# Mixer LayerNorm: fifth up chunk split ahead of the first normalization, the third tile's steps put between the h2 rests, rotary key of all tiles at once

## The chip, the cores and the metric

The kernel runs on one core of one Trainium2 chip. Its time is the device time of one execution in microseconds (us), the median of several runs. Before the change it is 981.97 us (3 runs, 981.78 to 982.18). The core has a matrix engine (PE, with its weight loads shown apart as PEld), a vector engine (DVE), a scalar engine (ACT), GpSimd (POOL), and SyncE (SP), which issues most of the loads. Each engine runs its own instructions strictly in order and waits on semaphores for the others.

## The reference, cut to what matters

One layer of a streaming encoder on a sequence of 512 positions and 1024 channels, all in float32:

```
h = layer_norm(x) * (1 + sc_t) + sh_t
y = token_mixer(h)              # pooling, latent attention and spatial gating, gated, merged, @ w_o
x = layer_norm(ALPHA * x + gt_t * y) * ln_t_g + ln_t_b      # "mixer's LayerNorm"
h = layer_norm(x) * (1 + sc_f) + sh_f                       # called h2 in the kernel
z = h @ w_up                    # 1024 -> 2 * 2816, then a convolution over 3 positions
y = (silu(gate) * val) @ w_down
x = layer_norm(ALPHA * x + gt_f * y) * ln_f_g + ln_f_b
```

sh, sc and gt come from a product of silu(c) with a weight w_ada. In the attention, a key of 64 channels per position (kr) is turned by rotary angles: the first half times cos minus the second times sin, and so on.

## The kernel before, in words

**Numbers.** A float32 product is made of three passes of a faster format: every operand a is split into a "high" part (ah, a cast on ACT) and a "rest" (al = a - ah, on DVE or POOL), and PE adds al*bh, ah*bl and ah*bh. Names end in h and l for the two. `wsplit` (L92, L93) does it for a weight chunk of 128x1024, `mm3` (L106 to L108) does the three products of one tile, `mm_chunk` (L113, L114, L116) those of a chunk of eight tiles. The 512 positions are four tiles t of 128 rows; the 1024 channels of h and h2 are eight column tiles j.

**Order.** A scheduler orders each engine's instructions from the program's order and estimated times. Where the order matters the code pins it: `tc.issue_after(ins)` keeps what follows behind an instruction, and `in_turn` chains steps on DVE one after another around the mixer's LayerNorm.

**Three places matter here.**

*Rotary key* (L549 to L603). After the first projection, for each tile t: ACT squares the latent columns (L553, L554), POOL takes the power -1/2 of the sums (`power`, L130 and L133, twice per tile), ACT scales by it (cn, L558, L559), DVE multiplies the key by cos and sin (tA, tB, L565, L568), and POOL makes the rotated key ro (L571, L572), its high part twice (L574, L575) and its rest (L576) in a tile kr of its own. Then PE transposes cn (ptc, L585) and kr (ptk, L597, L601) and begins the rotary queries (pq, L106 to L108).

*Row gate gt_t* (`ada_rows`, L815 to L829, called at L895). The modulation row gt_t is summed on DVE by `ada_piece` during the eight merges of the first branch. `ada_rows` splits the two sums (ACT L821, POOL L822) and lets PE spread each over all rows with two products (pgt, L827); DVE adds a bias row (L828), which SP loads. It is called right before the pooling products (pmx). The spatial gating's products follow, `uv_half(2)` and `uv_half(3)` (tiles pu, L929 to L932).

*Mixer's LayerNorm* (L1114 to L1345). `project_out` makes y for tile after tile (accumulators pyo) and calls `after_mixer(t)` behind each. For a tile: `residual` (DVE, adds ALPHA*x, takes statistics, L1196 to L1201), `centre` (L1208), `scale` (L1216), `second_stats` (the statistics for h2, DVE L153 and L142, then three small POOL steps, L130, L133, L145, that give rs), `second_norm` (ACT, xr, L1229). PE turns xr (`turn`, tiles pth, L1241), two tiles t at a time: the first pair's turns stand among the products of the fourth tile. `second_modulation(tp, jp)` makes two column tiles of h2 for a pair tp: ACT the high parts (h2T0h to h2T7h, L1260) and a full copy (h2f, L1263), DVE the rests (h2T0l to h2T7l, L1269).

Meanwhile the first six chunks of w_up are split early: `early_split(m)` casts (ACT, L1174; names uph, wuph), `early_low(m)` makes the rest (DVE, L1180; upl, wupl). `up_early` then multiplies these six chunks by the first pair of tiles (256 positions) as soon as h2 is there (tiles pzu, 128x256), and later by the second pair; the other 38 chunks follow in whole (128x512).

In `after_mixer` before, the fifth chunk (m = 4) is cast on ACT behind the second tile's xr, and its rest on DVE stands behind the second tile's statistics; the third tile's three steps come before the first rest h2T0l.

Of the kernel before, what the change touches and what calls it, by code (L numbers as in the profile page):

```python
# [8 lines left out]
F32 = mybir.dt.float32  # L9
F32R = mybir.dt.float32r  # L10
# [9 lines left out]
TT = 4  # L20
# [30 lines left out]
def trunk(ctx: ExitStack, tc: tile.TileContext, A, out):  # L51
# [498 lines left out]
    krs = []  # L550
    for t in range(TT):
        sq = pad_t("sq")
        nc.scalar.activation(sq[:, 0:256], lat[t][:, 0:256], AF.Square, accum_out=ss[:, t, 0:1])  # L553
        nc.scalar.activation(sq[:, 256:384], lat[t][:, 256:384], AF.Square, accum_out=ss[:, t, 1:2])  # L554
        power(rr[:, t, 0:1], ss[:, t, 0:1], 1.0 / 256.0, RMS_EPS, 1)
        power(rr[:, t, 1:2], ss[:, t, 1:2], 1.0 / 128.0, RMS_EPS, 1)
        cn = pt_t(f"cn{t}")
        nc.scalar.activation(cn[:, 0:256], lat[t][:, 0:256], AF.Copy, scale=rr[:, t, 0:1])  # L558
        nc.scalar.activation(cn[:, 256:384], lat[t][:, 256:384], AF.Copy, scale=rr[:, t, 1:2])  # L559
        cqn.append(cn)  # L560
        ro = sm.tile([P, 64], F32, name="ro", tag="ro", bufs=2)
        tA = sm.tile([P, 2, 32], F32, name="tA", tag="tA", bufs=2)
        tB = sm.tile([P, 2, 32], F32, name="tB", tag="tB", bufs=2)
        src = lat[t][:, 384:448].rearrange("p (a b) -> p a b", a=2)
        nc.vector.tensor_tensor(  # L565
            out=tA, in0=src, in1=cosT[:, t : t + 1, :].broadcast_to([P, 2, 32]), op=ALU.mult
        )
        nc.vector.tensor_tensor(  # L568
            out=tB, in0=src, in1=sinT[:, t : t + 1, :].broadcast_to([P, 2, 32]), op=ALU.mult
        )  # L570
        nc.gpsimd.tensor_tensor(out=ro[:, 0:32], in0=tA[:, 0, :], in1=tB[:, 1, :], op=ALU.subtract)  # L571
        nc.gpsimd.tensor_tensor(out=ro[:, 32:64], in0=tA[:, 1, :], in1=tB[:, 0, :], op=ALU.add)  # L572
        kr = act_t(f"kr{t}", F32)
        nc.gpsimd.tensor_copy(out=kr[:, 0:64].bitcast(F32R), in_=ro)  # L574
        nc.gpsimd.tensor_copy(out=kr[:, 64:128], in_=kr[:, 0:64])  # L575
        nc.gpsimd.tensor_tensor(out=kr[:, 128:192], in0=ro, in1=kr[:, 0:64], op=ALU.subtract)  # L576
        krs.append(kr)
    for m in range(2, 4):
        th0.append(gate(0, m))
    cT_hi = []  # L580
# [13 lines left out]
    krL = m_t("krL", F32R)  # L594
    pt = ps("ptk")
    for t in range(TT):
        nc.tensor.transpose(pt[:, t * P : (t + 1) * P], krs[t][:, 0:128], ident)  # L597
    nc.scalar.copy(out=krT, in_=pt)
    pt = ps("ptk")
    for t in range(TT):  # L600
        nc.tensor.transpose(pt[0:64, t * P : (t + 1) * P], krs[t][:, 128:192], ident)  # L601
    nc.vector.tensor_copy(out=krL[0:64, :], in_=pt[0:64, :])
    nc.gpsimd.memset(f(krL[64:128, :]), 0.0)  # L603

# [285 lines left out]
    for m in range(KT):  # L890
# [1 line left out]
            pool(m + 1)  # L892
        merge(0, m, oT_hi, oT_lo, th0[m])
        behind_split(ada_piece, 0, m)
    gt_t = ada_rows(0, 0, "gtt")  # L895

    mx_hi = []
    mx_lo = []
    for g in range(4):
# [43 lines left out]
        nc.vector.bn_stats(out=stv[:, q, 0, :], in_=v0[q])  # L943

    v0 = uv_half(2, "v", lambda q: behind_split(ada_piece, 1, q))
    v1 = uv_half(3, "v", lambda q: behind_split(v_second, q))
    shf = ada_cols(1, C_SHF, False, "shf")
    gsg = row_tiles(6, pt_t, "gsg")
# [282 lines left out]
            )  # L1231

    turned = {}

    def turn(tp, jp):
        pt = ps("pth")
# [10 lines left out]
    def second_modulation(tp, jp):  # L1247
        tt_ = slice(2 * tp * P, (2 * tp + 2) * P)
        pt = turned.pop((tp, jp))
        full = pad_t("h2f")  # L1250
        for jj in range(2):
            j = 2 * jp + jj
            c = slice(jj * 256, (jj + 1) * 256)
            if tp and jj:
                nc.vector.tensor_scalar(
                    out=h2_hi[j][:, tt_], in0=pt[:, c], scalar1=scf[:, j : j + 1],
                    scalar2=shf[:, j : j + 1], op0=ALU.mult, op1=ALU.add,
                )
            else:
                nc.scalar.activation(  # L1260
                    h2_hi[j][:, tt_], pt[:, c], AF.Identity, bias=shf[:, j : j + 1], scale=scf[:, j : j + 1]
                )
            nc.scalar.activation(  # L1263
                full[:, c], pt[:, c], AF.Identity, bias=shf[:, j : j + 1], scale=scf[:, j : j + 1]
            )
        for jj in range(2):
            j = 2 * jp + jj
            c = slice(jj * 256, (jj + 1) * 256)
            ins = nc.vector.tensor_tensor(  # L1269
                out=h2_lo[j][:, tt_], in0=full[:, c], in1=f(h2_hi[j][:, tt_]), op=ALU.subtract  # L1270
            )
        return ins
# [259 lines left out]
```

## Time and profile before

| what | value |
|---|---|
| median of 3 runs | 981.97 us |
| the profiled execution | 979.05 us |
| its span (first to last instruction) | 977.2 us |
| granted TensorE clock, mean over the span | 0.992 |
| PE busy | 957.4 us, 98% |
| DVE, ACT, POOL busy | 588.8, 388.8, 291.1 us |
| HBM read | 116.30 MB |

The profile is one execution. In a timeline a row gives start, duration, engine, line, operation, output and inputs, shape, and in brackets how long the engine sat idle before it and what ended that idle time. Matmul durations are modelled ends of pipelined work and overlap; the distance between two starts is what a matmul costs. The chain of work that ended last lies 85% on PE, 5% on DVE, 4% on POOL and 2% on ACT.

### The profile page before, as it was taken

How to read it: one execution, taken by the hardware profiler on the slowest of the kernel's cores; microseconds unless marked ns; L12 is line 12 of the kernel's file. 1: busy time of each engine (PE TensorE's matmuls, PEld its weight loads, DVE VectorE, ACT ScalarE, POOL GpSimd, SP SyncE). 2: the span in 40 equal slices, each digit the busy share in tenths (PEclk: the TensorE clock that was granted, in tenths of full speed). 3: DMA queues.
4: the chain of work that ended last, by engine and by line, in shares of the span. 5: the costliest groups of instructions: out<-in, count | busy, mean ns of one | idle time of the engine just before them, and what ended most of it. 6: DMA issues, size and time to landing. Idle time of an engine off the chain costs nothing.

```text
span 977.2 us, 12237 instructions
## 1 busy us (share of the span) xinstructions
PE 957.4 (98%) x4566; PEld 805.0 (82%) x4566; DVE 588.8 (60%) x899; ACT 388.8 (40%) x654; POOL 291.1 (30%) x295
## 2 busy tenths in 40 slices
PE   8999999999999999999999998999999999999996
PEld 7888888888878888888888887988888888888885
DVE  6958657546785665656533486595555565632367
ACT  4575656533233322422323235364444444422121
POOL 3773122122440031302012721121111121755654
PEclk9999999999999999999999999999999999999998
DMA  9712112134445533364243450034343433333222
GB/s 334 287 62 85 51 40 81 52 130 151 134 135 183 178 123 101 120 235 171 66 118 120 132 192 22 23 129 129 108 130 108 134 125 94 119 112 107 86 87 87
DMA packets 45708, 119.20 MB, mean 122 GB/s; under 512 B 5329, under 2 KB 8785, under 8 KB 45649
## 3 DMA queue, kind: packets, MB, share of 16 engines
q1 hardware_dynamic: 45216, 118.25, 37.2%
q8 instruction: 36, 0.59, 0.2%
q10 hardware_dynamic: 432, 0.17, 0.1%
q14 instruction: 24, 0.19, 0.1%
HBM read 116.30 MB, written 2.10 MB: 121 GB/s over the span
## 4 chain that ended last, share of the span: by engine, by line
PE 85%; DVE 5%; POOL 4%; ACT 2%; issue 2%; DMA 2%; DVEq 0%; POOLq 0%; SPq 0%
PE pzu L113 7%; PE pzu L114 7%; PE pzu L116 7%; PE pg L113 4%; PE py L113 4%; PE pg L114 4%; PE pg L116 4%; PE py L114 4%; PE py L116 4%; PE pyd L1138 3%; PE pyd L1135 3%; PE pyd L1137 3%; PE pu L932 3%; PE pu L931 3%; PE pu L929 3%; PE lat L508 2%
## 5 line engine op out<-in xcount | busy, mean ns | idle before, releaser
L93 DVE TENSOR_TENSOR wupl<-wup,wuph 128x1024 fp32r<-128x1024 f32 x38 | 48.2, 1269 | 71.0 <-PE pzu L116 44.7
L1104 POOL TENSOR_TENSOR d<-d,gtfb 128x512 f32<-128x512 f32 x44 | 73.9, 1700 | 37.6 <-DMA d<-in_wdn 35.8
L1386 POOL TENSOR_TENSOR zc<-zc 128x512 f32<-128x512 f32 x22 | 29.8, 1356 | 172.2 <-ACT zc L1385 152.6
L1109 DVE TENSOR_TENSOR dl<-d,dh 128x1024 fp32r<-128x1024 f32 x18 | 28.7, 1594 | 56.2 <-PE pyd L1135 50.9
L410 POOL TENSOR_TENSOR mg<-mg,th 128x512 f32<-128x512 f32 x16 | 31.3, 1958 | 92.5 <-DVE th L407 92.4
L92 ACT CAST wuph<-wup 128x1024 fp32r<-128x1024 f32 x38 | 39.9, 1050 | 46.5 <-PE pzu L114 46.5
L93 DVE TENSOR_TENSOR wgl<-wg,wgh 128x1024 fp32r<-128x1024 f32 x22 | 27.9, 1268 | 42.2 <-ACT wgh L92 29.5
L92 ACT CAST wbh<-wb 128x1024 fp32r<-128x1024 f32 x24 | 25.3, 1054 | 69.3 <-PE py L114 50.2
L809 DVE SCALAR_TENSOR_TENSOR ada<-adar,cact,ada 128x512 f32<-128x512 f32 x56 | 49.6, 917 | 0.8 <-DMA adar<-in_ada 0.8
L1108 ACT CAST dh<-d 128x1024 fp32r<-128x1024 f32 x18 | 19.0, 1053 | 62.5 <-PE pyd L1138 37.6
L1368 ACT ACTIVATE zc<-pzu,cols 128x512 f32<-128x512 f32 x44 | 34.2, 779 | 21.2 <-PE pzu L116 17.0
L92 ACT CAST wgh<-wg 128x1024 fp32r<-128x1024 f32 x22 | 23.3, 1057 | 40.3 <-PE pg L114 27.1
L93 DVE TENSOR_TENSOR wsgl<-wsg,wsgh 128x1024 fp32r<-128x1024 f32 x16 | 19.6, 1225 | 31.7 <-ACT wsgh L92 28.2
L93 DVE TENSOR_TENSOR wbl<-wb,wbh 128x1024 fp32r<-128x1024 f32 x24 | 30.5, 1271 | 9.7 <-ACT wbh L92 5.5
L92 ACT CAST wsgh<-wsg 128x1024 fp32r<-128x1024 f32 x16 | 16.9, 1053 | 48.6 <-PE pu L932 44.1
L1371 DVE SCALAR_TENSOR_TENSOR zc<-pzu,cols,zc 128x511 f32<-128x511 f32 x44 | 32.6, 743 | 4.1 <-ACT zc L1368 4.1
L730 POOL TENSOR_SCALAR pe<-pe,mx 128x128 f32<-128x128 f32 (+3 forms) x32 | 17.1, 537 | 54.9 <-DVE mx L729 54.5
L1375 DVE SCALAR_TENSOR_TENSOR zc<-pzu,cols,zc 128x510 f32<-128x510 f32 x44 | 32.6, 744 | 0.8
L1385 ACT ACTIVATE zc<-zc 128x512 f32<-128x512 f32 x22 | 13.9, 631 | 40.5 <-DVE zc L1375 40.4
L407 DVE SCALAR_TENSOR_TENSOR th<-th,py 128x512 f32<-128x512 f32 x16 | 11.0, 686 | 30.9 <-PE py L116 30.9
L862 POOL TENSOR_TENSOR asum<-apad 128x527 f32<-128x527 f32 x8 | 12.2, 1520 | 55.4 <-ACT apad L857 29.3
L294 DVE SCALAR_TENSOR_TENSOR acc<-ada,cact,acc 128x512 f32<-128x512 f32 (+1 forms) x27 | 26.9, 1011 | 0.7
(1431 smaller groups left out, 3138.3 us busy)
## 6 DMA issues: line engine op xcount, KB each, us to landing
wup<-in_wup SPq DMA_DIRECT2D x44, 512.0 KB, 3.6
adar<-in_ada SPq DMA_DIRECT2D x64, 256.0 KB, 3.9
wb<-in_wb SPq DMA_DIRECT2D x24, 512.0 KB, 3.6
wg<-in_wg SPq DMA_DIRECT2D x22, 512.0 KB, 3.6
d<-in_wdn SPq DMA_DIRECT2D x22, 512.0 KB, 3.6
wsg<-in_wsg SPq DMA_DIRECT2D x16, 512.0 KB, 3.7
ada<-in_ada1p SPq DMA_DIRECT2D x24, 256.0 KB, 5.0
x<-in_x SPq DMA_DIRECT2D x16, 256.0 KB, 3.4
```

Of the source, the lines that this page charges most:

```text
L92: nc.scalar.copy(out=hi[:, :n], in_=raw[:, :n])
L93: ins = nc.vector.tensor_tensor(out=lo[:, :n], in0=raw[:, :n], in1=f(hi[:, :n]), op=ALU.subtract)
L113: nc.tensor.matmul(o, wh[:, c], xl[k], start=k == 0, stop=False)
L114: nc.tensor.matmul(o, wh[:, c], xh[k], start=False, stop=False)
L116: nc.tensor.matmul(o, wl[:, c], xh[k], start=False, stop=k == KT - 1)
L410: nc.gpsimd.tensor_tensor(out=merged[m], in0=merged[m], in1=th, op=ALU.add)
L809: nc.vector.scalar_tensor_tensor(out=acc[n], in0=src, scalar=cact[:, k : k + 1], in1=acc[n], op0=ALU.mult, op1=ALU.add,)
L1104: nc.gpsimd.tensor_tensor(out=halves[n], in0=halves[n], in1=gt[n], op=ALU.mult)
L1368: nc.scalar.activation(t, pz, AF.Identity, bias=cols[:, cc + 3 : cc + 4], scale=cols[:, cc + 2 : cc + 3])
L1371: nc.vector.scalar_tensor_tensor(out=t[:, 1:512], in0=pz[:, 0:511], scalar=cols[:, cc + 1 : cc + 2], in1=t[:, 1:512], op0=ALU.mult, op1=AL ...
L1375: nc.vector.scalar_tensor_tensor(out=t[:, 2:512], in0=pz[:, 0:510], scalar=cols[:, cc : cc + 1], in1=t[:, 2:512], op0=ALU.mult, op1=ALU.add,)
L1386: nc.gpsimd.tensor_tensor(out=val, in0=val, in1=gate, op=ALU.mult)
```

## The change

It has four parts.

1. Rotary key: the powers are taken for two tiles at a time (columns of two tiles in one instruction), and the rotated key for all four tiles at once, in tiles `tA`, `tB`, `ro`, `kr`, `krl` of 512 columns, after the loop.
2. `ada_rows(0, ...)`, which makes gt_t, is called after `uv_half(2)` and no longer before the pooling products.
3. `early_split(4)` is called ahead of `second_norm(0)`.
4. The third tile's steps `residual` and `centre` stay behind its products; `scale` goes between the first and the second pair of h2 rests, `second_stats` behind the second pair; `second_norm(2)` and `early_split(5)` are kept behind the last full copy of the first pair of tiles.

```diff
+    tA, tB, ro, krl = (
+        act_t(name, F32)[:, : TT * 64].rearrange("p (t c) -> p t c", c=64)
+        for name in ("tA", "tB", "ro", "krl")
+    )
+    kr = act_t("kr", F32).rearrange("p (t c) -> p t c", c=128)
...
-        power(rr[:, t, 0:1], ss[:, t, 0:1], 1.0 / 256.0, RMS_EPS, 1)
-        power(rr[:, t, 1:2], ss[:, t, 1:2], 1.0 / 128.0, RMS_EPS, 1)
...
+        ts_ = slice(t - 1, t + 1)
+        power(rr[:, ts_, 0], ss[:, ts_, 0], 1.0 / 256.0, RMS_EPS, 2)
+        power(rr[:, ts_, 1], ss[:, ts_, 1], 1.0 / 128.0, RMS_EPS, 2)
...
+    nc.gpsimd.tensor_tensor(out=ro[:, :, 0:32], in0=tA[:, :, 0:32], in1=tB[:, :, 32:64], op=ALU.subtract)
+    nc.gpsimd.tensor_tensor(out=ro[:, :, 32:64], in0=tA[:, :, 32:64], in1=tB[:, :, 0:32], op=ALU.add)
+    nc.gpsimd.tensor_copy(out=kr[:, :, 0:64].bitcast(F32R), in_=ro)
+    nc.gpsimd.tensor_copy(out=kr[:, :, 64:128], in_=kr[:, :, 0:64])
+    nc.gpsimd.tensor_tensor(out=krl, in0=ro, in1=kr[:, :, 0:64], op=ALU.subtract)
...
         behind_split(ada_piece, 0, m)
-    gt_t = ada_rows(0, 0, "gtt")
...
     v0 = uv_half(2, "v", lambda q: behind_split(ada_piece, 1, q))
+    gt_t = ada_rows(0, 0, "gtt")
...
             in_turn(second_stats, t)
+            if t == 0:
+                early_split(4)
             second_norm(t)
         if t == 1:
-            early_split(4)
             in_turn(early_low, 4, nc.vector)
         if t == 2:
-            norm_steps(2)
+            in_turn(residual, 2)
+            in_turn(centre, 2)
         if t == 3:
             in_turn(second_modulation, 0, 0)
+            in_turn(scale, 2)
+            in_turn(second_modulation, 0, 1)
             in_turn(second_stats, 2)
-            for jp in (1, 2, 3):
+            for jp in (2, 3):
                 in_turn(second_modulation, 0, jp)
-            second_norm(2)
-            early_split(5)
+            with tc.issue_after(last_full[0]):
+                second_norm(2)
+                early_split(5)
```

What stands in the engines' queues: on DVE at the mixer's LayerNorm, before, from the third tile's statistics on (x_20 and x_21 are its two halves; the row with lntg is `centre`, with lntb `scale`):

```order
L1199 BN_STATS sto<-x_20_5106 128x6
L1199 BN_STATS sto<-x_21_5107 128x6
L1201 BN_AGGR mv<-sto 128x2
L1208 SCALAR_TENSOR_TENSOR x_20_5106<-x_20_5106,mv,lntg_5074 128x512
L1208 SCALAR_TENSOR_TENSOR x_21_5107<-x_21_5107,mv,lntg_5076 128x512
L1216 SCALAR_TENSOR_TENSOR x_20_5106<-x_20_5106,rs,lntb_5078 128x512
L1216 SCALAR_TENSOR_TENSOR x_21_5107<-x_21_5107,rs,lntb_5080 128x512
L1269 TENSOR_TENSOR h2T0l<-h2f,h2T0h 128x256
L1269 TENSOR_TENSOR h2T1l<-h2f,h2T1h 128x256
L153 BN_STATS st<-x_20_5106 128x6
L153 BN_STATS st<-x_21_5107 128x6
```

and now, in the same place:

```order
L1200 BN_STATS sto<-x_20_5068 128x6
L1200 BN_STATS sto<-x_21_5069 128x6
L1202 BN_AGGR mv<-sto 128x2
L1209 SCALAR_TENSOR_TENSOR x_20_5068<-x_20_5068,mv,lntg_5036 128x512
L1209 SCALAR_TENSOR_TENSOR x_21_5069<-x_21_5069,mv,lntg_5038 128x512
L1272 TENSOR_TENSOR h2T0l<-h2f,h2T0h 128x256
L1272 TENSOR_TENSOR h2T1l<-h2f,h2T1h 128x256
L1217 SCALAR_TENSOR_TENSOR x_20_5068<-x_20_5068,rs,lntb_5040 128x512
L1217 SCALAR_TENSOR_TENSOR x_21_5069<-x_21_5069,rs,lntb_5042 128x512
L1272 TENSOR_TENSOR h2T2l<-h2f,h2T2h 128x256
L1272 TENSOR_TENSOR h2T3l<-h2f,h2T3h 128x256
L153 BN_STATS st<-x_20_5068 128x6
```

The rests h2T0l and h2T1l have moved ahead of the two `scale` instructions, and the statistics behind two more rests.

On ACT in the same stretch, before (xr_5343 to xr_5409 are the first two tiles, uph_5414 the fifth chunk):

```order
L1174 CAST wuph<-wup 128x512 x4
L1229 ACTIVATE xr_5343<-x_00_5098,rs 128x512
L1229 ACTIVATE xr_5344<-x_01_5099,rs 128x512
L1229 ACTIVATE xr_5408<-x_10_5102,rs 128x512
L1229 ACTIVATE xr_5409<-x_11_5103,rs 128x512
L1174 CAST uph_5414<-wup 128x512
L1174 CAST uph_5415<-wup 128x512
L1260 ACTIVATE h2T0h<-pth,shfc,scfc 128x256
```

and now:

```order
L1175 CAST wuph<-wup 128x512 x4
L1175 CAST uph_5307<-wup 128x512
L1175 CAST uph_5308<-wup 128x512
L1230 ACTIVATE xr_5313<-x_00_5060,rs 128x512
L1230 ACTIVATE xr_5314<-x_01_5061,rs 128x512
L1230 ACTIVATE xr_5378<-x_10_5064,rs 128x512
L1230 ACTIVATE xr_5379<-x_11_5065,rs 128x512
L1262 ACTIVATE h2T0h<-pth,shfc,scfc 128x256
```

The two casts of the fifth chunk have moved ahead of the first tile's xr. Further on, the third tile's xr and the sixth chunk's casts have moved from between h2T5h and h2T6h to behind the copy that belongs to h2T7h.

On PE where the merges end (py) and the pooling products begin (pmx), before:

```order
L116 MATMUL py<-o7h,wbl 128x512
L827 MATMUL pgt<-adal,onesr 128x512
L827 MATMUL pgt<-adah,onesr 128x512
L827 MATMUL pgt<-adal,onesr 128x512
L827 MATMUL pgt<-adah,onesr 128x512
L106 MATMUL pmx<-po0l,wpoolh 128x512
```

and now:

```order
L116 MATMUL py<-o7h,wbl 128x512
L106 MATMUL pmx<-po0l,wpoolh 128x512 x2
L106 MATMUL pmx<-po2l,wpoolh 128x512 x2
L107 MATMUL pmx<-po0h,wpooll 128x512
L108 MATMUL pmx<-po0h,wpoolh 128x512
```

The four products of `ada_rows` have left this place: three of them now stand behind the first weight chunk of `uv_half(2)`, the fourth between `uv_half(2)` and `uv_half(3)`.

More of the change, by code (lines that the diff above doesn't have):

```diff
@@ L572, in trunk @@
[L572 to L577, printed above, removed]
+        src = lat[t][:, 384:448].rearrange("p (a b) -> p a b", a=2)
+        for dst, tab in ((tA, cosT), (tB, sinT)):
+            nc.vector.tensor_tensor(
+                out=dst[:, t, :].rearrange("p (a b) -> p a b", a=2), in0=src,
+                in1=tab[:, t : t + 1, :].broadcast_to([P, 2, 32]), op=ALU.mult,
+            )
@@ new lines, in trunk @@
+        if t % 2 == 0:
+            continue
+        ts_ = slice(t - 1, t + 1)
+        power(rr[:, ts_, 0], ss[:, ts_, 0], 1.0 / 256.0, RMS_EPS, 2)
+        power(rr[:, ts_, 1], ss[:, ts_, 1], 1.0 / 128.0, RMS_EPS, 2)
+        for u in (t - 1, t):
+            cn = pt_t(f"cn{u}")
+            nc.scalar.activation(cn[:, 0:256], lat[u][:, 0:256], AF.Copy, scale=rr[:, u, 0:1])
+            nc.scalar.activation(cn[:, 256:384], lat[u][:, 256:384], AF.Copy, scale=rr[:, u, 1:2])
+            cqn.append(cn)
@@ L596, in trunk @@
     for t in range(TT):
-        nc.tensor.transpose(pt[:, t * P : (t + 1) * P], krs[t][:, 0:128], ident)
+        nc.tensor.transpose(pt[:, t * P : (t + 1) * P], kr[:, t, :], ident)
     nc.scalar.copy(out=krT, in_=pt)
@@ L600, in trunk @@
     for t in range(TT):
-        nc.tensor.transpose(pt[0:64, t * P : (t + 1) * P], krs[t][:, 128:192], ident)
+        nc.tensor.transpose(pt[0:64, t * P : (t + 1) * P], krl[:, t, :], ident)
     nc.vector.tensor_copy(out=krL[0:64, :], in_=pt[0:64, :])
@@ L1233, in trunk @@
     turned = {}
+    last_full = []
     def turn(tp, jp):
```

18 lines of the change are left out of this document (2 added, 16 removed).

## The prediction

> **What bounds the kernel now.** I read the page's first part, then the waits of PE, then PE's timeline around the longest wait, then the timelines of the engines that end it.
>
> The page says that PE is busy nearly all of the span:
>
> ```profile
> PE 957.4 (98%) x4566; PEld 805.0 (82%) x4566; DVE 588.8 (60%) x899; ACT 388.8 (40%) x654; POOL 291.1 (30%) x295
> ```
>
> So only two things can shorten it: fewer or cheaper products, or a wait of PE that goes. The change removes no product. These are the waits of PE that concern it (total us, times, longest), in the order of the list:
>
> ```profile
> PE pzu L106 <- DVE h2T0l L1269: 4.5, 2, 4.1
> ...
> PE pgt L827 <- POOL adal L822: 1.1, 1, 1.1
> ...
> PE ptk L597 <- POOL kr L575: 0.2, 1, 0.2
> ```
>
> Each of the three belongs to one place of the change. The largest is between the mixer's last product and the first early up product:
>
> ```profile
> 597.85 0.39 PE L107 MATMUL pyo<-o7h,mgl 128*128 128x512 f32 x1
> 598.08 0.39 PE L108 MATMUL pyo<-o7h,mgh 128*128 128x512 f32 x1
> 602.61 0.38 PE L106 MATMUL pzu<-h2T0l,uph 128*128 128x256 f32 x1 [4.14 <-DVE h2T0l L1269]
> ...
> 603.66 0.41 PE L106 MATMUL pzu<-h2T0l,wuph 128*128 128x256 f32 x1
> 603.88 0.41 PE L107 MATMUL pzu<-h2T0h,wupl 128*128 128x256 f32 x1
> ...
> 607.77 0.28 PE L106 MATMUL pzu<-h2T2l,wuph 128*128 128x256 f32 x1
> 607.89 0.28 PE L107 MATMUL pzu<-h2T2h,wupl 128*128 128x256 f32 x1
> ```
>
> The wait has a second price. Behind it the products start 0.22 us apart, four microseconds later 0.12. The windows give the reason, the granted clock (the number behind POOL's):
>
> ```profile
> 603.00:604.00 1.00, 1.00 (x7) 1.00 (x7) 1.00 (x2) 0.00 (x0) 0.00 (x0) 0.55 0.00 0
> 604.00:605.00 1.00, 1.00 (x7) 1.00 (x6) 0.96 (x5) 0.00 (x0) 0.50 (x2) 0.50 0.00 0
> 605.00:606.00 1.00, 1.00 (x6) 1.00 (x6) 0.62 (x2) 0.21 (x1) 0.65 (x2) 0.50 0.00 0
> 606.00:607.00 1.00, 1.00 (x8) 1.00 (x8) 0.00 (x0) 1.00 (x2) 0.00 (x0) 0.74 0.00 0
> ```
>
> The missing clock sums to 0.45 + 0.50 + 0.50 + 0.26 = 1.7, so some 3.4 us ran at half speed. At 0.215 us each that is 16 products, each about 0.095 too long: 1.5 us.
>
> **Part 1: mixer's LayerNorm.** DVE's chain to h2T0l, and the later steps it is followed by:
>
> ```profile
> 591.90 0.21 DVE L142 BATCH_NORM_AGGREGATE mv<-st 128x2 f32<-128x12 f32 x1
> 595.49 1.29 DVE L1180 TENSOR_TENSOR upl<-wup,uph 128x512 fp32r<-128x512 f32 x2 [3.38 <-ACT uph L1174]
> 596.70 1.28 DVE L1196 SCALAR_TENSOR_TENSOR x<-x,pyo 128x512 f32<-128x512 f32 x2
> ...
> 600.82 1.40 DVE L1216 SCALAR_TENSOR_TENSOR x<-x,rs,lntb 128x512 f32<-128x512 f32 x2
> 602.14 0.41 DVE L1269 TENSOR_TENSOR h2T0l<-h2f,h2T0h 128x256 fp32r<-128x256 f32 x1
> ...
> 610.54 1.28 DVE L1196 SCALAR_TENSOR_TENSOR x<-x,pyo 128x512 f32<-128x512 f32 x2
> ...
> 617.29 0.21 DVE L142 BATCH_NORM_AGGREGATE mv<-st 128x2 f32<-128x12 f32 x1
> ```
>
> DVE stands idle for 3.38 us, because the fifth chunk's cast waits on ACT behind xr. With the cast moved ahead of the first xr, upl starts when the statistics end, at 592.11. It takes 1.21 (595.49 to 596.70), so the third tile starts at 593.32. Its residual, statistics and centre take 4.12 (596.70 to 600.82): 597.44. Now h2T0l stands there, ahead of scale (1.32, 600.82 to 602.14), and ends at 597.85. That is 4.70 earlier: 3.38 from the cast and 1.32 from scale.
>
> What else h2T0l needs comes from ACT:
>
> ```profile
> 586.59 1.52 ACT L1229 ACTIVATE xr<-x,rs 128x512 f32<-128x512 f32 x2 [7.88 <-POOL rs L145]
> 593.42 1.52 ACT L1229 ACTIVATE xr<-x,rs 128x512 f32<-128x512 f32 x2 [5.31 <-POOL rs L145]
> ...
> 595.88 0.56 ACT L1260 ACTIVATE h2T0h<-pth,shfc,scfc 128x256 fp32r<-128x256 f32 x1
> ...
> 600.85 0.60 ACT L1263 ACTIVATE h2f<-pth,shfc,scfc 128x256 f32<-128x256 f32 x1
> ...
> 619.47 1.52 ACT L1229 ACTIVATE xr<-x,rs 128x512 f32<-128x512 f32 x2 [9.30 <-POOL rs L145]
> ```
>
> The moved cast fits into the 7.88 idle us ahead of the first xr; behind it in ACT's queue stands only that xr, and its load was issued when an early raw buffer came free, so SP's queue keeps its order. The second xr came 1.52 behind the start of its statistics' last step (591.90 to 593.42), with DVE idle beside POOL. Now upl runs there, as it does behind the last tile's statistics, where the same way took 2.18 (617.29 to 619.47). So xr starts at 594.08 and ends at 595.60, and h2T0h stays near 595.88, now behind the turns instead of the cast. From there ACT steps by 0.452 (eleven steps to 600.85): the copy that h2T0l reads ends at 596.9, before 597.44.
>
> PE could start at 598.31, a product's 0.23 (597.85 to 598.08) behind its last. With h2T0l at 597.85 nothing is waited for: 602.61 - 598.31 = **4.3 us**, and the slow clock goes with it, **1.5 us**. A rule speaks on that second term. The Trainium skill, "TensorE: Matmul & The Clock Gate", Part 1, says that the gate watches free-running windows of about 3.4 us, so that one kernel may show 6, 11 or 14 slow products. By it the timed runs would hold 0.6 to 1.3 us for this term (at 0.095 each, an estimate), and the sum would be 0.2 to 0.9 smaller; the trace shows one case, 16.
>
> What is late next? In its new queue PE takes 24 products at 0.12 before h2T2l (601.2), 52 before h2T4l (604.5), 72 before h2T7l (606.9). DVE has them by about 600.0, 602.3 and, behind ACT's sixteenth step (595.88 + 15 x 0.452 + 0.56 = 603.2), 603.7. Here the held-back xr and the sixth chunk's casts help: before, they stood ahead of h2T6h. The last tile then starts at about 603.7 instead of 610.54, so its xr comes at 619.47 - 6.8 = 612.7, its first half at 613.4. PE reaches the turns of it
>
> ```profile
> 620.35 0.87 PE L1241 MATMUL pth<-ident,xr 128*128 128x128 f32 x6
> ```
>
> at 598.31 + (620.35 - 602.61) - 1.5 = 614.5, still behind. The second wait of the list (4.5 - 4.1 = 0.4) follows these turns through ACT and DVE, and stays. Part 1: 5.8 us.
>
> **Part 2: the row gate.** PE's third product of it waits for POOL:
>
> ```profile
> 287.85 0.40 PE L827 MATMUL pgt<-adah,onesr 128*128 128x512 f32 x1
> 289.33 0.49 PE L827 MATMUL pgt<-adal,onesr 128*128 128x512 f32 x1 [1.08 <-POOL adal L822]
> ```
>
> It could have started at 288.08, so **1.25 us** goes (1.08 by the modelled end); the four products remain, in places tens of us behind their operands. The cost that may come: ten accumulators (4 + 2 + 4) now stand in eight banks, so the last of `uv_half(3)` needs a bank that the first evictions of `uv_half(2)` on ACT free:
>
> ```profile
> 322.57 0.39 PE L931 MATMUL pu<-wsgh,hT0l 128*128 128x512 f32 x1
> ```
>
> ```profile
> 317.39 1.23 DVE L93 TENSOR_TENSOR wsgl<-wsg,wsgh 128x1024 fp32r<-128x1024 f32 x1 [2.89 <-ACT wsgh L92]
> ```
>
> ```profile
> 323.33 2.07 ACT L936 ACTIVATE v<-pu 128x512 f32<-128x512 f32 x4
> ```
>
> `uv_half(3)` begins at 322.57. The first of the four evictions ends near 323.9 (2.07 for four, one behind the other), and that accumulator's products stand 19 products on in PE's new queue: 322.57 + 19 x 0.23 = 326.9. Cost 0, at worst 0.3 if the bank is one that a later eviction frees. On DVE the first bias addition queues ahead of the weight rest at 317.39, which had 2.89 us of idle time ahead of it; behind it wait that rest and then PE. SP's two bias loads stand between two weight loads; behind them in SP's queue waits a load for a chunk that PE reaches later. Both are covered.
>
> **Part 3: the rotary key.**
>
> ```profile
> 72.12 0.38 PE L597 MATMUL ptk<-ident,kr 128*128 128x128 f32 x2
> ...
> 73.23 0.33 PE L597 MATMUL ptk<-ident,kr 128*128 128x128 f32 x1 [0.21 <-POOL kr L575]
> ...
> 73.61 0.93 PE L106 MATMUL pq<-wqrl,cT0h 128*128 128x512 f32 x3
> 74.38 0.40 PE L107 MATMUL pq<-wqrh,cT0l 128*128 128x512 f32 x1
> ```
>
> Eight turns at about 0.11 would end near 73.0; they end at 73.61. POOL's bounds are these:
>
> ```profile
> 66.84 0.26 POOL L571 TENSOR_TENSOR ro<-tA,tB 128x32 f32<-128x32 f32 x1
> ...
> 79.43 0.74 POOL L628 TENSOR_TENSOR qro<-qtA,qtB 128x256 f32<-128x256 f32 x1 [5.40 <-DVE qtB L620]
> ```
>
> The first ro stood behind 16 power steps, now behind fewer, so not after 66.84. The five joined steps have at most 256 columns, at most 0.74 each: 3.7, done by 70.5, ahead of 72.12. What comes next is cT0l:
>
> ```profile
> 73.01 0.74 DVE L124 SCALAR_TENSOR_TENSOR cT0l<-ptc,cols,cT0h 128x512 fp32r<-128x512 f32 x1
> ```
>
> It ends at 73.75, so 74.38 becomes about 73.8: **0.55 us**, with bounds 0 (the next chain waits elsewhere) and 0.6. Against the joining speaks the Trainium skill, "SBUF — State Buffer", "Who interferes with whom": a DVE step with two inputs in SBUF and a POOL step that reads SBUF exclude each other. By it POOL may lose two weight rests of 1.2, done by 73.0; then the sum has 0 here.
>
> **The sum.** 4.3 + 1.5 + 1.25 + 0.55 = 7.6 us off the profiled execution's 979.05 (its span, and 1.85 around it that the change doesn't touch): 971.45. The median of the runs is 2.92 above that execution; I keep this distance: 981.97 - 7.6 = **974.4 us**.
>
> **The rivals.** *The start is only partly closed.* PE's queue holds the turns of the second xr among the mixer's last products. If POOL's rs comes later than 2.18 behind DVE, PE waits at these turns and h2T0l slips with it. The margin is 598.31 - 597.85 = 0.46. With up to 2 us left and no slow clock: 976.4. For it speaks the small margin; against it the like case at 617.29.
>
> *The slow clock costs less in the timed runs.* If it fell 8 products shorter there, 8 x 0.095 = 0.75 is not to be had: 975.1. Beside it stands the rule cited above (the Trainium skill, "TensorE: Matmul & The Clock Gate", Part 1). The window from 603 has 0.55, so the clock fell inside it, not at the restart at 602.61: its fall isn't tied to the wait's end. For the forecast speaks that the runs agree within 0.4 us.
>
> *The change doesn't do it at the LayerNorm.* If h2T0l stays later than about 3 us, the clock drops as well, and only parts 2 and 3 remain, 1.8: 980.2. Against it: both DVE terms are plain in the queue.
>
> *Slower: the last tile becomes the bound.* Its chain now starts behind all sixteen ACT steps. If its xr comes L later than 614.5 allows, PE idles at the turns and pays the slow clock again: -7.6 + L + 1.5. From L = 8.1 on, 2 us are lost: 984. This would need ACT's steps to be held by copies that DVE frees late. The margin is 1.1.
>
> **How the numbers follow.** Forecast 0.66, partly closed 0.16, shorter slow clock 0.08, nothing at the LayerNorm 0.06, slower 0.04. The forecast's own range is 974.0 to 975.4 (part 3 at 0, part 2 at 0.3 less), below it 973.4 if the 0.4 wait goes too and the clock term is 1.7. The range takes in the first two rivals: 973.4 to 977.0. A measurement of this kernel can tell about 0.2%, 2 us, from no change: the first three cases are faster by more (0.90), the fourth is within (0.06), the last slower (0.04).
>
> **What would show it.** In the changed profile: no PE wait above 0.5 us at h2T0l's first product, granted clock 1.00 in every window from there on, that product 0.2 to 0.3 behind the mixer's last; upl directly behind the statistics on DVE; no wait of pgt on adal and of ptk on kr. Wrong would be: a new PE wait at the turns (pth), at `uv_half(3)`'s last accumulator, or at upl of the sixth chunk; or these waits gone and the time not.

## The result, and the profile after

The changed kernel takes 973.0 us (median of 4 runs, 971.64 to 974.8) against 981.88 us for the kernel before (4 runs, 981.01 to 982.18): a ratio of 0.9909 with a 95% interval of 0.9892 to 0.9925, so it is faster, as forecast. The forecast was 974.4 with a range from 973.4: the median lies 1.4 below the forecast and 0.4 below the range. The profiled execution took 973.34 us, its span is 971.6.

From PE's list of waits after the change (total us, times, longest), behind a wait of 4.4 at the start that both kernels have:

```profile
...
PE pqn L106 <- ACT wqk3h L688: 0.9, 1, 0.9
PE g0ps L443 <- DMA ada<-in_ada: 0.7, 1, 0.7
PE pqn L106 <- ACT wqk6h L688: 0.5, 1, 0.5
PE pzu L106 <- DVE h2T0l L1272: 0.4, 1, 0.4
```

All three waits that the change was about are gone: of h2T0l only the 0.4 of the second pair is left, and pgt and ptk stand no longer in the list. In their place stand waits at the start and in the attention (g0ps, wqk3h), far from any edit, and the one at wqk6h has grown from 0.3 to 0.5; they come back below. PE's timeline at the mixer's LayerNorm:

```profile
595.39 1.58 PE L1243 MATMUL pth<-ident,xr 128*128 128x128 f32 x12
...
598.42 0.39 PE L108 MATMUL pyo<-o7h,mgh 128*128 128x512 f32 x1
598.64 0.28 PE L106 MATMUL pzu<-h2T0l,uph 128*128 128x256 f32 x1
598.76 0.28 PE L107 MATMUL pzu<-h2T0h,upl 128*128 128x256 f32 x1
...
614.82 0.82 PE L1243 MATMUL pth<-ident,xr 128*128 128x128 f32 x6
```

The first up product starts 0.22 behind the mixer's last, and the next 0.12 behind it: full speed. The windows (granted clock behind POOL's number) say the same where 0.50 stood before:

```profile
603.00:604.00 1.00, 1.00 (x10) 1.00 (x10) 0.59 (x2) 1.00 (x2) 0.26 (x1) 1.00 0.00 0
604.00:605.00 1.00, 1.00 (x11) 1.00 (x10) 1.00 (x3) 1.00 (x3) 0.00 (x0) 1.00 0.00 0
605.00:606.00 1.00, 1.00 (x11) 1.00 (x10) 1.00 (x3) 0.89 (x2) 0.00 (x0) 1.00 0.09 16
```

DVE's chain, then ACT's:

```profile
592.34 0.21 DVE L142 BATCH_NORM_AGGREGATE mv<-st 128x2 f32<-128x12 f32 x1
592.47 1.25 DVE L1181 TENSOR_TENSOR upl<-wup,uph 128x512 fp32r<-128x512 f32 x2
...
597.72 0.42 DVE L1272 TENSOR_TENSOR h2T0l<-h2f,h2T0h 128x256 fp32r<-128x256 f32 x1
...
603.75 1.28 DVE L1197 SCALAR_TENSOR_TENSOR x<-x,pyo 128x512 f32<-128x512 f32 x2
```

```profile
594.53 1.52 ACT L1230 ACTIVATE xr<-x,rs 128x512 f32<-128x512 f32 x2 [5.97 <-POOL rs L145]
...
612.68 1.52 ACT L1230 ACTIVATE xr<-x,rs 128x512 f32<-128x512 f32 x2 [6.79 <-POOL rs L145]
```

upl stands right behind the statistics, and the second xr comes 2.19 behind their last step (592.34 to 594.53), where 2.18 was forecast. The last tile starts at 603.75 (forecast 603.7) and its xr at 612.68 (forecast 612.7). At the row gate and the rotary key:

```profile
288.98 0.39 PE L116 MATMUL py<-o7h,wbl 128*128 128x512 f32 x1
289.20 0.62 PE L106 MATMUL pmx<-po0l,wpoolh 128*128 128x512 f32 x2
```

```profile
73.05 0.60 PE L599 MATMUL ptk<-ident,kr 128*128 128x128 f32 x4
73.48 0.60 PE L603 MATMUL ptk<-ident,krl 128*64 128x128 f32 x4
73.84 0.94 PE L106 MATMUL pq<-wqrl,cT0h 128*128 128x512 f32 x3
74.62 0.39 PE L107 MATMUL pq<-wqrh,cT0l 128*128 128x512 f32 x1
```

To add up the edits I take, for each PE product that stands in both profiles, its start after minus its start before, and the median of that over a stretch. It is 0.93 at 61 to 70 us (ahead of every edit), 0.27 at 76 to 88, 1.58 at 230 to 280, 0.22 at 340 to 420 and at 560 to 590, -5.60 at 645 to 700, -5.64 at the end. The steps between these are what each stretch cost or gained:

| profile | start | rotary key | attention | row gate | LayerNorm | all |
|---|---|---|---|---|---|---|
| changed kernel | +0.93 | -0.66 | +1.31 | -1.36 | -5.82 | -5.64 |
| forecast | 0 | -0.55 | 0 | -1.25 | -5.8 | -7.6 |

The edits bring 0.66 + 1.36 + 5.82 = 7.8 us, 0.2 more than forecast. The 2.24 us lost at the start and in the attention, where both kernels run the same instructions, hide a part of it in this pair of profiles; yet the medians stand 8.9 apart (the interval of the ratio is 7.4 to 10.6 us). So the profiles and the medians disagree on something that is not the change. The experiments were made for that, and to test each step by itself.

### The profile page after: what moved, and what is told of

It reads as the page before. It is cut to its first block, busy times and chain, and to the rows that moved or that the text cites. A ratio compares the mean times of both kernels' runs of the same rounds, so it can differ in the third digit from the quotient of the medians.

```text
span 971.6 us, 12209 instructions
## 1 busy us (share of the span) xinstructions
PE 955.5 (98%) x4566; PEld 803.9 (83%) x4566; DVE 587.9 (61%) x899; ACT 388.6 (40%) x654; POOL 287.1 (30%) x272
## 4 chain that ended last, share of the span: by engine, by line
PE 95%; DMA 2%; ACT 1%; POOL 1%; DVE 1%; issue 0%; SPq 0%; DVEq 0%; POOLq 0%
PE pzu L116 7%; PE pzu L113 7%; PE pzu L114 7%; PE py L113 4%; PE py L114 4%; PE py L116 4%; PE pg L113 4%; PE pg L116 4%; PE pg L114 4%; PE pyd L1138 3%; PE pyd L1136 3%; PE pyd L1139 3%; PE pu L931 3%; PE pu L932 3%; PE pu L929 3%; PE lat L508 2%
```

## The experiments

The ratio is always against the kernel before, timed beside it on the same chip.

**The kernel before, once more.** No edit.

> The kernel before, unchanged, profiled once more. Theory A (the profiled execution of before was an early one: its loads at the start and the chunk wqk3 came up to 2.2 us sooner than in most executions): the new profile starts its steady work about 1 us later or waits about 1 us for a wqk load, and its span is 978 to 981 us; PE's wait for h2T0l is again 4.1 us and the sum of missing clock behind it again 1.7. Theory B (in the timed executions the wait at the mixer's LayerNorm and the slow clock behind it are longer than in the profile): same start as in the first profile, and more missing clock behind 603 us or elsewhere.

982.21 us (980.41 to 983.3), ratio 1.0013 (1.0002 to 1.0025): the same code comes out 1.3 us slower than itself, and the interval doesn't hold 1. So a timed difference of one or two us below shows little by itself. The new profile is 3.2 us longer than the first: +2.61 at the start, +0.2 in the attention, +0.30 at the LayerNorm. Its windows at the start and behind the LayerNorm's wait:

```profile
15.00:20.00 5.00, 5.00 (x20) 3.92 (x20) 4.50 (x10) 2.40 (x6) 1.99 (x3) 0.52 1.03 379
20.00:25.00 5.00, 5.00 (x26) 4.44 (x26) 4.86 (x5) 2.13 (x6) 3.49 (x3) 0.80 1.05 380
...
605.00:610.00 5.00, 4.23 (x23) 4.23 (x24) 3.75 (x10) 1.05 (x2) 1.15 (x3) 0.66 0.00 0
```

The same two windows of the start in the first profile:

```profile
15.00:20.00 5.00, 5.00 (x19) 3.71 (x19) 5.00 (x8) 3.88 (x8) 3.61 (x4) 0.66 1.05 380
20.00:25.00 5.00, 5.00 (x31) 4.31 (x30) 4.82 (x6) 2.96 (x6) 2.45 (x3) 1.00 1.06 382
```

There 0.34 x 5 = 1.7 us of clock are missing, which is 3.4 us at half speed; here 0.48 x 5 + 0.20 x 5 = 3.4, twice that. Theory A holds: the execution that I predicted from was an early one. Of the 79 runs of the kernel before that were timed beside these experiments and beside the change, 6 took 979.05 us or less; their median is 980.99, and they lie between 978.59 and 983.91.

**The LayerNorm edits alone.**

```diff
+            if t == 0:
+                early_split(4)
             second_norm(t)
...
+            in_turn(scale, 2)
+            in_turn(second_modulation, 0, 1)
```

> Before, with the LayerNorm edits alone. Theory A: 5.8 us faster than before (5.0 to 6.8), profile without PE's 4.1 us wait and with granted clock 1.00 from 598 to 608. Theory B: the LayerNorm is worth more than its profile says, 7 us or more. Theory C (the rotary and row gate edits shift loads and this is where the rest came from): 5.8 us here, and more than 1.9 us from the other two.

972.94 us (972.66 to 973.35), ratio 0.9918 (0.9902 to 0.9934), which is 8.0 us (6.5 to 9.6). Its profile gains 5.94 at the LayerNorm. The timed gain is more than theory A allowed for (5.0 to 6.8), as theory B said, though its interval reaches down to 6.5. The timed runs don't show what the other two edits add to it: the whole change lies at 972.51 over nine runs, 0.4 below this median, where the profiles give the two 2.0.

**The row gate alone.**

```diff
-    gt_t = ada_rows(0, 0, "gtt")
...
     v0 = uv_half(2, "v", lambda q: behind_split(ada_piece, 1, q))
+    gt_t = ada_rows(0, 0, "gtt")
```

> Before, with ada_rows(0) behind uv_half(2) alone. Theories A and B: 1.25 to 1.4 us faster, no wait of pgt, none at the last accumulator of uv_half(3). Theory C: over 1.8 us.

Ratio 0.9986 (0.9974 to 0.9998), 1.4 us (0.2 to 2.5), which by itself tells none of the theories apart; the profile has -1.36 at this place, and no wait at `uv_half(3)`. It has a wait of 0.7 at wqk3h, like the changed kernel.

**The rotary key alone.**

```diff
-        power(rr[:, t, 0:1], ss[:, t, 0:1], 1.0 / 256.0, RMS_EPS, 1)
+        power(rr[:, ts_, 0], ss[:, ts_, 0], 1.0 / 256.0, RMS_EPS, 2)
...
+    nc.gpsimd.tensor_copy(out=kr[:, :, 0:64].bitcast(F32R), in_=ro)
```

> Before, with the joined rotary key alone. Theories A and B: 0.5 to 0.7 us faster, turns of kr end 0.7 us earlier against the turns of cn. Theory C: over 1 us faster, or slower if the later loads (wqk3) come late because of it: a wait of about 0.9 us at wqk3h as in the changed kernel.

Ratio 0.9981 (0.9969 to 0.9992), 1.9 us (0.8 to 3.0); the profile has -0.68 at this place. The timed figure is theory C's (over 1 us), but the same code twice gave 1.3 us, and the three parts timed alone would add up to 11.3, more than the whole change gives; so I don't read more into it. What this profile shows beside is theory B's mechanism:

```profile
599.15 0.39 PE L108 MATMUL pyo<-o7h,mgh 128*128 128x512 f32 x1
604.11 0.58 PE L106 MATMUL pzu<-h2T0l,uph 128*128 128x256 f32 x1 [4.57 <-DVE h2T0l L1271]
```

```profile
600.00:605.00 5.00, 0.89 (x4) 0.89 (x5) 4.93 (x11) 2.96 (x7) 1.05 (x2) 0.69 0.18 70
605.00:610.00 5.00, 5.00 (x30) 5.00 (x30) 2.09 (x6) 2.71 (x5) 1.15 (x3) 0.62 0.00 0
```

Here the slow clock began inside the wait, at 601.9, and held until 608.75: 0.31 x 5 + 0.38 x 5 = 3.4 us of clock are missing, against 1.7 in the first profile. In the four profiles with the LayerNorm's old order and its full wait (the first, its repeat, the row gate alone, the rotary key alone) the LayerNorm costs 0, 0.30, 0.53 and 0.94 more than in the first, 0.44 on average. Only a small part of that is the clock. In the repeat the wait itself is 0.3 longer (4.45); with the row gate alone the turns of the last tile's xr come 0.5 later, with a wait of 0.33; here the wait is 0.43 longer, and since 2.2 us of the two slow stretches lay within it, the second one cost about 0.5. Against the average of the four, the LayerNorm's removal is worth nearer to 6.3 than to 5.8.

**The changed kernel, once more.** No edit.

> The changed kernel, unchanged, profiled once more. Theory D (executions differ by themselves in three places: the slow clock of the start lasts one or two stretches of 3.4 us, the slow clock behind the wait at the LayerNorm likewise, and the chunk wqk3 lands up to 1.2 us late): the median is 971.5 to 974, and the wait at wqk3h (0.9 in the changed profile) comes or doesn't, whatever the edits. Theory E (moving the row gate's products makes the load of wqk3 land late, 4.7 to 4.9 us from issue in place of 3.4 to 3.9): the wait of 0.7 to 0.9 at wqk3h is there again.

972.33 us (970.65 to 972.77), ratio 0.9921 (0.9907 to 0.9934). In this profile the edits give the same: -0.68, -1.36, -5.80. But the start is 1.03 earlier than in the first profile of before, not 0.93 later, and the attention costs 0.60, not 1.31 (the wait at wqk3h is 0.3). Its start never had the slow clock:

```profile
15.00:20.00 5.00, 4.93 (x28) 3.74 (x28) 4.96 (x9) 3.89 (x8) 3.34 (x4) 1.00 1.06 383
20.00:25.00 5.00, 5.00 (x29) 4.29 (x29) 4.82 (x6) 4.03 (x8) 3.55 (x4) 1.00 1.06 380
```

Theory D holds for the start. Over all 14 profiles, the two above and the twelve of these experiments, the start varies by 3.65 us, from -1.03 to +2.62, and it goes with the slow clock between 14 and 22 us: this profile has none, eight have one stretch of 3.4 us (-0.24 to +1.04), five have two (+1.60 to +2.62). A later single stretch, between 28 and 36 us, is in all of them but this one.

**The changed kernel with the row gate in its old place.**

```diff
+    gt_t = ada_rows(0, 0, "gtt")
     mx_hi = []
...
-    gt_t = ada_rows(0, 0, "gtt")
```

> The changed kernel with ada_rows(0) put back in its old place: rotary and LayerNorm edits stay. Theory D: 1.36 us slower than the changed kernel, 7.3 to 8.5 us faster than before, the wait at wqk3h comes or doesn't. Theory E: no wait at wqk3h, its load lands 3.4 to 3.9 us from issue, and the kernel is only 0.2 to 0.7 us slower than the changed one.

972.75 us (970.84 to 974.07), ratio 0.9927 (0.9914 to 0.994). PE has no wait at wqk3h, as theory E wants it, and the median is 0.4 above the changed kernel's, which is theory E's number and not theory D's 1.36. But a kernel without the gate's move (the next but one) loses 0.62 at that place, with a landing of 4.34 us, and one with it (the old place of xr, below) loses nothing, with a landing of 3.64. So the move is neither needed for the late landing nor enough for it, and theory E falls as it was put. Of the four profiles with the move and the old loads, three land at 4.26, 4.66 and 4.87, and of the eight without it all but one between 3.39 and 4.03; whether the move makes it more frequent stays open. New here is a wait where the forecast had its first rival, at the turns of the second xr:

```profile
595.30 1.58 PE L1244 MATMUL pth<-ident,xr 128*128 128x128 f32 x12 [0.42 <-ACT xr L1231]
```

The LayerNorm gains 5.25 in this profile, not 5.8. In the changed kernel's own two profiles the same place costs PE 0.13 and 0.15.

**The cast alone.** Before, with `early_split(4)` moved ahead of the first `second_norm` and nothing else.

```diff
+            if t == 0:
+                early_split(4)
             second_norm(t)
         if t == 1:
-            early_split(4)
```

> Before, with early_split(4) ahead of second_norm(0) and nothing else: h2T0l 3.4 us earlier, so PE waits 0.8 us for it in place of 4.1. Theory F (the slow clock comes only behind a long idle time of PE): granted clock 1.00 from 598 to 610 and 4.9 us faster than before, in executions with two slow stretches up to 6. Theory G (any idle time of PE at this place, or the kind of work there, brings the slow clock): a slow stretch of 3.4 us stays and the kernel is 3.4 us faster.

Ratio 0.9965 (0.9955 to 0.9976), 3.4 us; 2.94 at the LayerNorm in the profile. The timed gain is the number of theory G, but the clock is that of theory F:

```profile
PE pzu L106 <- DVE h2T0l L1269: 1.1, 2, 0.7
...
PE pzu L107 <- DVE upl L1180: 1.0, 1, 1.0
...
PE pth L1241 <- ACT xr L1229: 0.5, 1, 0.5
```

The wait for h2T0l is down to 0.7 and the granted clock stays at 1.00 in every window of 1 us from 596 to 640, but PE then arrives too early at the sixth chunk's rest and at the last tile's turns. Those 1.5 us behind the front are what was not foreseen here.

**The order among the rests**, with the fifth chunk's cast in its old place. The edit also holds the third tile's xr and the sixth chunk's casts behind the last full copy.

```diff
+            in_turn(scale, 2)
+            in_turn(second_modulation, 0, 1)
             in_turn(second_stats, 2)
...
-            second_norm(2)
-            early_split(5)
+            with tc.issue_after(last_full[0]):
+                second_norm(2)
+                early_split(5)
```

> Before, with the order of the third tile's steps among the rests alone, the fifth chunk's cast in its old place: h2T0l 1.3 us earlier, PE waits 2.8 us in place of 4.1. Theory F with a bound above 2.8 us: clock 1.00 and 2.8 us faster. Theory F with a bound below 2.8, or theory G: slow stretch stays and 1.3 us faster.

Ratio 0.9981 (0.997 to 0.9992), 1.9 us; 1.59 in the profile.

```profile
604.02 0.39 PE L106 MATMUL pzu<-h2T0l,uph 128*128 128x256 f32 x1 [2.58 <-DVE h2T0l L1271]
```

The wait is 2.6, and a slow stretch of 3.4 us follows (0.66 in the window from 605). So a wait of 2.6 brought the slow clock; 0.7 didn't.

**PE kept busy during the wait.** Before, with 16 products that nobody reads.

```diff
+    warm = ps("warm")
+    for i in range(16):
+        nc.tensor.matmul(warm, early[0][0][0][:, 0:P], mg_hi[i % KT], start=True, stop=True)
     up_early((0, 1), 0)
```

> Before, with 16 more products of 128x512 into an accumulator that nobody reads, put into PE's queue between the mixer's last product and the first early up product; h2T0l is as late as before. They fill 16 x 0.227 = 3.6 of the 4.1 us that PE waits. Theory F (the slow clock comes from PE standing idle): granted clock 1.00 behind the wait, the first up product at the same distance from the mixer's last (4.5 us), and 1.5 us faster than before in the profile between 590 and 640 us. Theory G (the slow clock comes from the kind of work there, or from its beginning): a slow stretch of 3.4 us stays, no gain.

980.84 us, ratio 1.0003 (0.9991 to 1.0015): no gain. The clock did what theory F says, 1.00 in every window from 596 to 610, so it was PE standing idle that brought it down. The products behind it came 1.5 us sooner, and then PE gave it back (the profile even loses 0.4 at the LayerNorm):

```profile
PE pzu L107 <- DVE upl L1180: 1.0, 1, 1.0
PE pzu L106 <- DVE h2T0l L1269: 0.8, 2, 0.4
...
PE pth L1241 <- ACT xr L1229: 0.5, 1, 0.5
```

In the old order the slow clock cost nothing of its own: the sixth chunk's rest and the last tile's xr were due at that time anyway. In the first profile this xr's first half, all that the next turns need, ended at 620.28, and the turns started at 620.35.

**The third tile's xr and the sixth chunk's casts in their old place.** Else as changed.

```diff
-            for jp in (2, 3):
-                in_turn(second_modulation, 0, jp)
+            in_turn(second_modulation, 0, 2)
             with tc.issue_after(last_full[0]):
                 second_norm(2)
                 early_split(5)
+            with tc.issue_after(last_cast[0]):
+                in_turn(second_modulation, 0, 3)
```

> The changed kernel with the third tile's xr and the sixth chunk's casts put back between h2T5h and h2T6h on ACT; all else as changed. My reading of the changed trace (that the hold keeps the last tile off the path): h2T6h comes behind them at about 605.9 in place of 601.4, h2T7l ends 4.4 us later, the last tile starts 4.4 us later, its xr ends at 618.6, and the turns, which stand at 614.8, wait: with a margin of 0.6 the kernel loses 3.8 us between 600 and 640 us, 1.5 more if one of the waits is long enough for the slow clock (over 0.7, at most 2.6 us). Rival (the hold is only tidiness, since PE has 40 more products to run): no wait above 0.5, no loss.

975.79 us (973.92 to 977.46), ratio 0.995 (0.9931 to 0.9968). The LayerNorm gains 2.41 in place of 5.82: 3.4 lost, where 3.8 was expected.

```profile
615.61 0.39 PE L107 MATMUL pzu<-h2T0h,upl 128*128 128x256 f32 x1 [2.12 <-DVE upl L1182]
617.83 0.87 PE L1244 MATMUL pth<-ident,xr 128*128 128x128 f32 x6 [0.53 <-ACT xr L1231]
```

The sixth chunk's rest takes the first 2.1 of it, the turns the rest. The expectation's margin of 0.6 was taken from the end of both halves of xr; the turns need the first half, which in the changed profile ends at 613.50, 1.3 ahead of them. Set against the products ahead of the LayerNorm, this half comes 4.6 later here, and the turns 3.3.

A wait of 2.1 did not bring the slow clock here, and one of 2.6 did. What divides them can be read from windows cut where the clock changes, at times that the trace holds. Within each execution all its changes lie on one grid of 3.413 us (in the first profile the slow stretches begin at 16.01, 29.66 and 603.10, which are 4 and 172 steps apart). On that grid, first the order among the rests, then this kernel, then the rotary key alone (PE's busy time follows the length of the window):

```profile
601.81:605.22 3.41, 1.20 (x10) 1.20 (x11) 3.34 (x8) 3.41 (x9) 1.69 (x2) 1.00 0.12 49
605.22:608.64 3.42, 3.42 (x19) 3.42 (x18) 3.39 (x10) 0.85 (x2) 0.73 (x2) 0.50 0.00 0
```

```profile
611.91:615.32 3.41, 1.58 (x14) 1.34 (x12) 3.38 (x7) 0.00 (x0) 0.30 (x2) 1.00 0.00 0
615.32:618.74 3.42, 2.61 (x20) 2.41 (x21) 0.84 (x2) 1.77 (x3) 1.43 (x3) 1.00 0.44 117
```

```profile
598.51:601.92 3.41, 1.03 (x5) 0.52 (x3) 3.34 (x7) 3.41 (x9) 0.83 (x2) 1.00 0.48 154
601.92:605.33 3.41, 1.22 (x5) 1.22 (x6) 3.41 (x7) 1.04 (x3) 0.22 (x1) 0.50 0.00 0
605.33:608.75 3.42, 3.42 (x17) 3.42 (x17) 1.76 (x6) 1.46 (x3) 1.15 (x3) 0.50 0.00 0
```

PE idle for 2.2 us of a step brought half speed in the next one, 1.8 didn't. The wait of 4.57 fell on two steps with 2.4 and 2.2 of idle time, and so it brought two slow stretches. Around the LayerNorm no profile breaks this line: the other slow stretches follow steps with 2.9, 3.4 and 2.9 us idle, and no step with 1.2 or less is followed by one.

**Attention loads one head earlier.** Else as changed.

```diff
+        if h + 2 < H:
+            load_attention_weights(h + 2)
         if h + 1 < H:
             attention_weights(h + 1)
```

> The changed kernel with each attention chunk's load (wqk) issued one head earlier, so that it stands ahead of a weight load instead of behind one. Theory D (its landing varies by itself and PE pays for it when it is late): no PE wait at wqk3h, none or 0.2 less at wqk6h; 0.2 to 1.3 us off the profile at 120 to 190 us against the changed kernel's two profiles, 0.3 to 1 us off the median, which may drown in the spread of the runs (2 us for one kernel). Rival: the load ahead makes the weight chunk behind it late, and a wait of the same length appears at a gate chunk.

971.44 us (969.67 to 972.52), ratio 0.9903 (0.9886 to 0.9921). The attention costs 0.42 less than in the first profile of before, where the changed kernel's two profiles have 1.31 and 0.60 more; no PE wait at a wqk chunk is left, and none came at a gate chunk, so the rival falls. The median lies 1.1 below that of the changed kernel's nine runs, which weren't timed beside it, so the gain is shown in the profile alone. The chunk's load (wqk3) still stands behind a weight load in SP's queue, issued at 105.66 behind one at 105.28, and takes 3.9 us; what helps is that it is issued 14 us earlier. The cast of wqk3h, which had waited for its load in the changed kernel (first row; 1.20 in the repeat), finds it landed (second row, this kernel):

```profile
125.01 0.51 ACT L688 CAST wqk3h<-wqk 128x384 fp32r<-128x384 f32 x1 [1.81 <-DMA wqk<-in_wqk]
...
118.69 0.50 ACT L694 CAST wqk3h<-wqk 128x384 fp32r<-128x384 f32 x1
```

**The fifth chunk's rest behind the third tile's statistics**, on top of that.

```diff
-        if t == 1:
-            in_turn(early_low, 4, nc.vector)
         if t == 2:
             in_turn(residual, 2)
+            in_turn(early_low, 4, nc.vector)
             in_turn(centre, 2)
```

> The kernel with the early attention loads, and the fifth chunk's rest (early_low(4)) behind the third tile's statistics instead of ahead of its residual. Theory H (the second xr comes 2.19 us behind its statistics, not 1.52, because the chunk's rest reads two tiles of SBUF on DVE while POOL makes rs; the residual, which reads PSUM, leaves POOL alone): the second xr starts 1.5 to 1.6 us behind the last step of its statistics, PE's turns of it never wait (0.42 us in one profile of the changed order), h2T0l ends at the same place, and LayerNorm's share between 585 and 645 us is 5.8 to 6.0 us off the kernel before. Rival (POOL's three steps take longer by themselves there): 2.2 us again.

970.17 us (969.69 to 970.84), ratio 0.9892 (0.9873 to 0.9911): the lowest median of the study. DVE's step and ACT's:

```profile
588.89 0.21 DVE L142 BATCH_NORM_AGGREGATE mv<-st 128x2 f32<-128x12 f32 x1
589.02 1.23 DVE L1207 SCALAR_TENSOR_TENSOR x<-x,pyo 128x512 f32<-128x512 f32 x2
```

```profile
590.42 1.52 ACT L1240 ACTIVATE xr<-x,rs 128x512 f32<-128x512 f32 x2 [5.32 <-POOL rs L145]
```

xr comes 1.53 behind the statistics, not 2.19, and PE doesn't wait at the turns: theory H. The rule is the one the forecast weighed at the rotary key (the Trainium skill, "SBUF — State Buffer", "Who interferes with whom"): a DVE step with two inputs in SBUF holds up POOL's reads, one with a single SBUF input, outside the two-port modes, doesn't. These two orders agree with it: 0.66 us for three tiny POOL steps, of which the first two take 0.53 and 0.88 beside the chunk's rest in the changed profile and 0.19 and 0.55 beside the residual here. The LayerNorm's share is 5.93, as without this edit, so against the attention loads alone the timed gain (ratio intervals overlap) isn't shown.

## Why the prediction was right and where it failed

**The step that failed** is the one from the profile to the runs: "The median of the runs is 2.92 above that execution; I keep this distance: 981.97 - 7.6 = 974.4". With it the profiled execution drops out of the sum, and the forecast rests on 981.97, the median of three runs. I took these three for the kernel's level because they agree within 0.4 us. That was luck: the kernel before spreads over 5.3 us (978.59 to 983.91 in 79 runs), and its median is 980.99, 1.0 lower. The 2.92 was two draws from this spread, the profiled execution 1.9 below the median and the three runs 1.0 above it. From 980.99 the forecast's own 7.6 gives 973.4, and the 7.8 measured in the profiles 973.2, beside 973.0 and 972.33 measured; what is left of the miss is within the spread of the runs. The range had terms for each edit and none for that spread. Its ends aren't what its terms add up to either: 974.4 + 0.55 + 0.3 is 975.25 and not 975.4, and 974.4 - 0.4 - 0.2 is 973.8 and not 973.4, so by its own terms the range would have missed by more.

**The slow clock**, 1.5 us: right in this profile, open for the runs. The forecast's second rival held that it might fall shorter there. In no profile did it: five have the wait of 2.6 us or more, four have one stretch of 3.4 us behind it and one has two. The rule weighed there (the Trainium skill, "TensorE: Matmul & The Clock Gate", Part 1) names free-running windows of 3.4 us, and stretches of that length are what the traces show, on one grid per execution; that a wait may bring two of them was not considered. It explains little of the 0.44 above, though: the second stretch cost about 0.5 in one profile of four, 0.1 on average, and the rest is longer waits. With the 0.44 the profiles' 7.8 becomes 8.3, against 8.5 between the medians of all runs (980.99 of 79, 972.51 of 9); no run shows what the clock did at this place in the timed executions. The third rival's condition, that the clock drops if h2T0l stays later than about 3 us, was set too high: a wait of 2.58 brought it.

**The front of the LayerNorm**, 4.3: right. h2T0l started 4.06 behind the mixer's last product before and starts 0.70 ahead of it now, 4.76 earlier where 4.70 was forecast. The "2.18" for the second xr was right to 0.01.

**Its back**: right, and more important than I made it. I named the margin at the turns as 1.1; it is 1.3 (xr's first half ends at 613.50, the turns that need it start at 614.82), where before it was 0.07. PE kept busy in the old order shows that a front 1.5 us earlier is worth nothing without an earlier back, and the old place of xr and casts shows that the hold, with the other edits in place, is worth 3.4 of the 5.8. The mechanism of the "slower" rival exists, with 1.3 of room to the other side.

**"The start is only partly closed"**: happened, but small. At the turns of the second xr PE lost 0.13 and 0.15 in the changed kernel's two profiles, 0.4 with the old place of xr and the casts, and 0.7 with the gate in its old place (idle for 0.42): at most a third of the 2 us that I gave it.

**The row gate**: 1.36, forecast 1.25; no cost at `uv_half(3)`'s accumulators, as worked out. **The rotary key**: 0.66 to 0.70, forecast 0.55 with an upper bound of 0.6; kr's turns now pass in 0.8 us (73.05 to 73.84), 0.1 less than forecast. The bound was the end of cT0l, which I left where it was; set against the products ahead of the edits it comes 0.2 earlier too. And two of POOL's five joined steps took 1.4 and 1.7 us, not 0.74 at most; they still ended 3.6 us ahead of kr's turns.

**What stays open.** What decides how many slow stretches the start has (none, one or two) wasn't tried; PE is busy in the steps ahead of them, so the idle time that explains the LayerNorm's doesn't explain these. The six profiles with the whole LayerNorm change lie between -1.03 and +1.04 there, the other eight between 0 and +2.62, although the LayerNorm's edits stand more than 500 us behind the start; I take this for chance, and no run here proves it. What the row gate and the rotary key are worth rests on the aligned profiles, which agree within 0.1 us; the timed runs are too far spread for it.

## What to carry to other kernels

A single profiled execution and a median of three runs are two draws from the same spread: set the sum of the edits against a median of many runs, and give the range a term of its own for the spread, here a microsecond. Align two profiles instruction by instruction and look at the stretches: that separates 0.1 us of an edit from 3 us of luck in code that did not change. When a wait at the front of a chain goes, follow the same chain to its end before booking the gain: here the back was due 1.5 us later, and only the second half of the change made room for it.

## What the runs showed of the hardware

- The slow clock came in stretches of 3.4 us on one grid per execution. Around the LayerNorm a step of the grid was slow when PE had been idle for 2.2 us or more of the step before, and not with 1.8 or less: one stretch behind a wait of 2.58, two behind one of 4.57 that fell on two steps, none behind one of 2.12.
- At the start it came with PE busy in 5.00 of 5 us (window from 15, granted clock 0.52): two stretches in five executions, one in eight, none in one.
- A load of 192 KB issued behind one of 512 KB landed 3.4 to 4.9 us after its issue in executions of nearly the same code; issued 14 us earlier, again behind such a load, it took 3.9 us and PE no longer waited for it.
- Two POOL steps of 128x1 took 0.53 and 0.88 us beside a DVE step with two inputs in SBUF, 0.19 and 0.55 beside one with one input in SBUF and one in PSUM.
